# Two column blocks of the third gate among the first projections, and a new place for the modulation's multiply-adds

## The chip, the cores and the metric

One core of a Trainium2 chip runs the whole layer in one launch. The metric is device time in microseconds. TensorE (PE) multiplies and writes to PSUM, VectorE (DVE) and ScalarE (ACT) work elementwise, GpSimd (POOL) does small things, and SyncE (SP) issues nearly all loads.

## The reference

One decoder layer on 256 tokens of width 2048, all in float32. The conditioning vector `c` gives six modulation vectors; the residual stream is normed, scaled and shifted to `h`, and one wide projection of `h` feeds three token mixers and three gates:

```python
mod = (jax.nn.silu(c) @ w_ada[l] + b_ada[l]).reshape(B, N_MOD, 1, D)
sh1, sc1, gt1, sh2, sc2, gt2 = (mod[:, j] for j in range(N_MOD))
h = rmsnorm(x, g_mix[l]) * (1.0 + sc1) + sh1
z = h @ w_in[l]
(mq, mk, mv, mo, mi, mf, dq, dk, dv, sq, sk, sv, gm, gd, gs) = split_cols(z, IN_SIZES)
...
merged = (jax.nn.sigmoid(gm) * (out_m @ w_branch[l, 0])
          + jax.nn.sigmoid(gd) * (out_d @ w_branch[l, 1])
          + jax.nn.sigmoid(gs) * (out_s @ w_branch[l, 2]))
x = x + gt1 * (merged @ w_out[l])
...
x = x + gt2 * ((jax.nn.silu(gate) * hid[..., D_FF:]) @ w_down[l])
```

`gs`, 2048 columns wide, is the third gate: it weighs the stick-breaking branch. `h` needs the first two modulation vectors, `sh1` and `sc1`, and so 2048 x 4096 numbers of `w_ada` (33.6 MB) ahead of the first whole projection.

## The kernel before

**Exact products.** A float32 factor is split into a high part (a cast on ACT) and a low part (a subtraction on DVE); each product is three matmuls, high x high, high x low and low x high. `weights` (L338) loads a raw chunk of up to four k tiles (128 rows each) by 512 columns, 1 MB, casts `hi` (L349) and subtracts `lo` (L351), two k tiles at a time. `gemm` (L357) runs over chunks and calls `tick` (L209) between them. Raw chunks come from a pool of three buffers, with a fourth added while `state["spare"]` is set (`raw_tile`, L217); the modulation's raw tiles come from the same pool.

**The modulation as partial sums.** Because `h` for a k tile needs only its own rows of `sh1` and `sc1`, the vectors are made in portions: two k tiles, two more (`ada_first`, L259), then three quads of four (`ada_quad`, L280). In a portion DVE multiplies rows of `w_ada` by the conditioning value and adds them up (`ada_mac`, L225: L230 starts a sum, L232 adds), PE sums over partitions (L248), and `make_h` (L465) scales the normed `x` to `h` on ACT and splits it. These steps are generators in the queue `ada`: each `next` is one step, and in a quad one step is one multiply-add of 128 x 1024.

**The first projections.** Thirteen column blocks (`first`, L515) are worked on with whatever k tiles of `h` exist: `visit(cis, kt1, rate)` (L568) brings each block in `cis` up to k tile `kt1` by `partial` (L528). A block begun before is copied back from SBUF into PSUM ("put", L545) or its new sum is added by DVE (L558); a piece not finished is copied out (L556). Blocks 0 and 1 stay in PSUM (`kept`). `rates["ada"]` and `rates["side"]` say how many steps of each queue a tick runs; `partial` also runs steps until the `h` that it needs has been made. After the visits come the last k tiles of each block (L901), with stick-breaking in the queue `side` after block 5; then the third gate's four column blocks by `gates` (L857), two before and two after the drain of that queue.

**What sets the order.** Loads go out on SP in the order of the program. On PE, DVE and ACT the framework places instructions by a simulated timeline, with program order as priority; `tc.issue_after(ins)` puts the block's instructions behind `ins` on its engine. `state["split"]` is the latest low-part subtraction in program order, `state["load"]` the latest weight load. `ada_late` (L294) already puts its multiply-adds behind `state["split"]`.

Of the kernel before, what the change touches and what calls it, by code (L numbers as in the profile page):

```python
# [10 lines left out]
F32 = mybir.dt.float32  # L11
F32R = mybir.dt.float32r
AF = mybir.ActivationFunctionType
# [4 lines left out]
P = 128  # L18
S = 256
# [16 lines left out]
C_GM, C_GD, C_GS = 10248, 12296, 14344  # L36
# [3 lines left out]
def kernel(  # L40
# [14 lines left out]
    adap = ctx.enter_context(tc.tile_pool(name="adap", bufs=3))  # L55
# [7 lines left out]
    def slot(i, name):  # L63
        n = NT * MH * (MDH + 1) + 8 if i == 2 else 2048
        return slots.tile([P, n], F32, tag=f"s{i}", name=name)
# [4 lines left out]
    def wide(name):  # L70
        return tmp.tile([P, 512], F32, tag="wide", name=name, bufs=3)

    def sidewide(name):
        return tmp.tile([P, 512], F32, tag="sidewide", name=name, bufs=4)

    def small(name):
        return tmp.tile([P, 256], F32, tag="small", name=name, bufs=3)

    V, A, T = nc.vector, nc.scalar, nc.tensor
# [111 lines left out]
    side = deque()  # L191
    ada = deque()
    state = {"ada": 0.0, "side": 0.0, "split": None, "load": None, "hold": None, "h": 0, "spare": None}
# [13 lines left out]
    rates = {"ada": 0.0, "side": 1.0}  # L207

    def tick():  # L209
        for key, queue in (("ada", ada), ("side", side)):  # L210
            state[key] += rates[key]
            n = int(state[key])
            state[key] -= n
            pump(queue, n)
# [10 lines left out]
    def ada_mac(accs, raw, kt0, nk):  # L225
        for k in range(nk):
            kt = kt0 + k
            acc = accs[kt % len(accs)]
            if kt < len(accs):
                V.tensor_scalar(acc, raw[:, k, :], ccol[:, kt:kt + 1], None, ALU.mult)  # L230
            else:
                state["mac"] = V.scalar_tensor_tensor(acc, raw[:, k, :], ccol[:, kt:kt + 1], acc, ALU.mult, ALU.add)  # L232
# [47 lines left out]
    def ada_quad(k0, acc):  # L280

        for q in range(8):
            raw = raw_tile(2, 1024, "raw4")
            for i in range(2):
                r0, c0 = q * 256, i * D + k0 * P
                with tc.issue_after(state["load"].ins):
                    nc.sync.dma_start(raw[:, :, i * 512:(i + 1) * 512],
                                      w_ada[r0:r0 + 256, c0:c0 + 512].rearrange("(k p) f -> p k f", p=P))
            for k in range(2):
                ada_mac([acc], raw[:, k:k + 1, :], 2 * q + k, 1)  # L290
                yield
        ada_sums([acc], k0, 4)

# [38 lines left out]
    a1 = const.tile([P, KD], F32, name="a1")  # L332
    b1 = const.tile([P, KD], F32, name="b1")
# [89 lines left out]
    def split(hi, lo, src):  # L423

        A.copy(hi, src)  # L425
        return V.tensor_tensor(lo, src, hi.bitcast(F32), ALU.subtract)


    h1 = [slots.tile([P, KD // 2, 2 * S], F32R, tag=t, name="h1") for t in ("hh", "hl")]
# [3 lines left out]
    xnT_k = lambda kt: xnT[kt // 8][:, (kt % 8) * S:(kt % 8 + 1) * S]  # L433
# [29 lines left out]
            A.copy(xnT[k2 // 4][:, (k2 % 4) * 512:(k2 % 4 + 1) * 512], pb)  # L463

    def make_h(kt0, kt1):  # L465
        ts = []
        for kt in range(kt0, kt1):
            t = small("ht")
            ts.append(t)
            hi, lo = hact[0](kt), hact[1](kt)  # L470
            if kt0 == 0:
                A.activation(hi, xnT_k(kt), AF.Identity, scale=a1[:, kt:kt + 1], bias=b1[:, kt:kt + 1])
                V.tensor_scalar(t, xnT_k(kt), a1[:, kt:kt + 1], b1[:, kt:kt + 1], ALU.mult, ALU.add)
                state["split"] = V.tensor_tensor(lo, t, hi.bitcast(F32), ALU.subtract)
            else:
                A.activation(t, xnT_k(kt), AF.Identity, scale=a1[:, kt:kt + 1], bias=b1[:, kt:kt + 1])
                state["split"] = split(hi, lo, t)
        if kt0 == 0:
            state["first"] = state["split"]
        state["h"] = kt1  # L480
# [19 lines left out]
    def dest_D(i):  # L500
        def f(b):
            pieces = []
            for lo_, hi_, t in ((0, 8, None), (8, 1032, dq), (1032, 2056, dk), (2056, 3080, dv)):
                s_, e_ = max(lo_, i * 440), min(hi_, (i + 1) * 440)
                if s_ >= e_:
                    continue
                if t is None:
                    d = zif[:, b, s_:e_]
                else:
                    d = t[:, b * MW + s_ - lo_:b * MW + e_ - lo_]  # L510
                pieces.append((slice(s_ - i * 440, e_ - i * 440), d))
            return pieces
        return f

    first = []  # L515
# [5 lines left out]
        first.append(("T", C_SV + ch * 512, 512, dest_T(sv, ch), 1.0))  # L521
    for i in range(7):
        first.append(("T", C_IF + 440 * i, 440, dest_D(i), 1.0))

    def shaped(src, dst):
        return src.rearrange("p (a b) -> p a b", a=dst.shape[1]) if len(dst.shape) == 3 else src

    def partial(ci, kt0, kt1):  # L528
        orient, col0, n, dest, scale = first[ci]
        while state["h"] < kt1:  # L530
            pump(ada, 1)
        if kt0 == 0 and ci == 0:
            state["first"], done = state["mac0"], state["first"]
        pin = kt0 == 0 and ci < 2
        if kt0 == 0 and ci < 2:
            kept[ci] = [bank("kept"), bank("kept")]
        acc = kept.get(ci)


        put = acc is None and 0 < kt0 and kt1 < KD and not (kt1 == 4 and ci in (6, 8))  # L540
        if put:
            acc = [gp.tile([P, 512], F32, tag="gp", name="gp") for _ in range(2)]
            for b in range(2):
                for cs, d in dest(b):
                    A.copy(shaped(acc[b][:, cs], d), d)  # L545
        acc = gemm(orient, hact, w_in, 0, col0, n, kt0, kt1, hold=state["first"] if pin else None, hold_all=pin,
                   acc=acc)
        if kt0 == 0 and ci == 0:
            state["first"] = done
        for b in range(2):  # L550
            for cs, d in dest(b):
                if ci in kept:
                    if kt1 == KD:
                        A.activation(d, shaped(acc[b][:, cs], d), AF.Copy, scale=scale)
                elif put or kt0 == 0:
                    A.copy(d, shaped(acc[b][:, cs], d))  # L556
                else:
                    V.scalar_tensor_tensor(d, shaped(acc[b][:, cs], d), scale, d, ALU.mult, ALU.add)  # L558
        tick()

    kept = {}
# [1 line left out]
    quads = slot(4, "quads")  # L563
    ada.append(ada_first(2))
    ada.extend(ada_quad(k0, quads[:, (i % 2) * 1024:(i % 2 + 1) * 1024]) for i, k0 in enumerate((4, 8, 12)))
    done = [0] * 13

    def visit(cis, kt1, rate):  # L568
        rates["ada"] = rate
        for ci in cis:  # L570
            partial(ci, done[ci], kt1)
            done[ci] = kt1

    visit(range(0, 9), 2, 0.62)
    visit(range(9, 13), 4, 1.9)
    visit(range(0, 9), 4, 1.0)
    side.append(late_vectors())
    rates["side"] = 0.4
    visit(range(0, 10), 8, 1.72)
    visit(range(10, 13), 12, 1.36)  # L580
    visit(range(0, 7), 12, 1.36)
    drain(ada)
    drain(side)
    state["spare"] = None
# [270 lines left out]
    mg = []  # L855

    def gates(col_g, ch, dst):  # L857
        acc = gemm("T", hact, w_in, 0, col_g + ch * 512, 512, 0, KD)
        for tt in range(NT):
            A.activation(dst[tt], acc[tt], AF.Sigmoid)  # L860
        tick()

    def mg_of(ch):
        o = (ch % 2) * 512
        return [mg[ch // 2][:, tt * 1024 + o:tt * 1024 + o + 512] for tt in range(NT)]
# [31 lines left out]
        yield from ada_columns(4, bsc2_c, a2, gffn_c)  # L897

    ada.append(ada_rest())
    rates["side"] = 2.4  # L900
    for ci in range(13):  # L901
        partial(ci, done[ci], 16)
        if ci == 5:
            side.append(stick())


    rates["side"] = 2.0
    rates["ada"] = 0.9
    mg.append(slot(8, "mg0"))
    for ch in range(2):  # L910
        gates(C_GS, ch, mg_of(ch))
    drain(side)
    mg.append(slot(9, "mg1"))
    side.append(diff())
# [8 lines left out]
    for ch in range(2):  # L923
        acc = gemm("T", hact, w_in, 0, C_MO + ch * 512, 512, 0, KD)
# [6 lines left out]
    for ch in range(2):  # L931
        acc = gemm("T", hact, w_in, 0, C_MV + ch * 512, 512, 0, KD)
# [5 lines left out]
    for t, col0, f0 in ((mqT, C_MQ, 0), (mkT, C_MK, 8)):  # L938
        for ch in range(2):
            acc = gemm("H", h1act, w_in, 0, col0 + ch * 512, 512, 0, KD)  # L940
# [44 lines left out]
    for ch in range(4):  # L985
        acc = gemm("T", mact, w_out, 0, ch * 512, 512, 0, KD)
        cs = slice(ch * 512, (ch + 1) * 512)
        for tt in range(NT):
            t = wide("t512")
# [15 lines left out]
        for tt in range(NT):  # L1005
# [5 lines left out]
            with tc.issue_after(m.ins) if last else nullcontext():  # L1011
                for i in range(4):
                    k = 4 * ch + i
                    m = T.transpose(pbs[i // 2][:, (i % 2) * S + tt * P:(i % 2) * S + (tt + 1) * P],
                                    x2[tt][:, k * P:(k + 1) * P], ident)
        for i in range(4):
            k = 4 * ch + i
# [13 lines left out]
    k = 0  # L1031
    while k < KD:
# [4 lines left out]
        for j in range(m):  # L1037
            b = b2[:, k + j:k + j + 1]
            hi, lo = h2act(k + j)[:, 0:S], h2act(k + j)[:, S:2 * S]
# [9 lines left out]
    for half, (c0, c1) in enumerate(((0, 6), (6, NCH))):  # L1049
# [37 lines left out]
        for n in range(4):  # L1087
            acc = gemm("T", act, w_down, c0 * 512, n * 512, 512, 0, 4 * (c1 - c0))
# [37 lines left out]
```

## Time and profile before

| | |
|---|---|
| median of 3 runs | 1785.43 us (1785.31 to 1785.56) |
| profiled execution | 1786.68 us |
| its span | 1785.0 us |
| PE busy | 1762.3 us (99%) |
| DVE busy | 1302.2 us (73%) |
| ACT busy | 954.2 us (53%) |
| HBM read | 419.68 MB, 236 GB/s over the span |

The span runs from the first to the last instruction of the profiled execution. Busy time of PE is a union of matmuls with modelled ends. DVE and ACT are no bound by their totals; what they hold up is read where PE waits.

### The profile page before, as it was taken

The numbers are of one execution on the slowest core, as the hardware profiler recorded it, in microseconds if no ns is written. First come the engines' busy times: TensorE is split into PE (matmuls) and PEld (weight loads), VectorE is DVE, ScalarE is ACT, GpSimd is POOL, SyncE is SP. The second block draws the span as 40 slices with busy tenths as digits, with TensorE's granted clock in tenths as the row PEclk, the third lists the DMA queues.
The fourth block names the chain that finished last, engine by engine and source line by source line (L and its number), as shares of the span: only waits on it lengthen the run. The fifth ranks groups of instructions, "written<-read, shape, count | busy, mean of one in ns | idle before, by whom it ended". The sixth has DMA issues, their size and how long they took to land.

```text
span 1785.0 us, 23783 instructions
## 1 busy us (share of the span) xinstructions
PE 1762.3 (99%) x9168; PEld 1514.4 (85%) x9168; DVE 1302.2 (73%) x1734; ACT 954.2 (53%) x1338; POOL 16.7 (1%) x44
## 2 busy tenths in 40 slices
PE   7989999999999999999999999999999999999998
PEld 6889999888778888888888888888888888888887
DVE  6878656888878688777986577888875556666654
ACT  6667555676566566544444555555553345555432
POOL 2000000000000000000000000000000000000000
PEclk9999999999999999999999999999999999999999
DMA  9989755867767667688996557777765555555563
GB/s 330 361 315 336 281 175 166 281 223 250 252 232 260 212 219 252 230 281 285 323 307 212 185 165 247 258 258 268 267 202 201 191 189 189 189 189 189 189 214 116
DMA packets 219730, 423.33 MB, mean 237 GB/s; under 512 B 9026, under 2 KB 31674, under 8 KB 219104
## 3 DMA queue, kind: packets, MB, share of 16 engines
q1 hardware_dynamic: 217328, 417.44, 68.6%
q0 software_dynamic: 1008, 2.23, 0.4%
q10 hardware_dynamic: 1280, 2.14, 0.3%
q8 instruction: 72, 1.18, 0.3%
q14 instruction: 42, 0.34, 0.1%
HBM read 419.68 MB, written 2.10 MB: 236 GB/s over the span
## 4 chain that ended last, share of the span: by engine, by line
PE 96%; DMA 2%; DVE 1%; ACT 0%; issue 0%; SPq 0%; DVEq 0%
PE gp L398 55%; PE acch L384 32%; PE gp L403 2%; PE kept L403 2%; DMA raw<-in_w_ada_dram 1%; PE psc L688 1%; DMA raw<-in_w_in_dram 0%; PE pm L248 0%; DVE quads L232 0%; SPq L271 0%; PE pr L329 0%; DVE lo L351 0%; PE pa L713 0%; PE pm L238 0%; PE pmg L886 0%
## 5 line engine op out<-in xcount | busy, mean ns | idle before, releaser
L351 DVE TENSOR_TENSOR lo<-raw,hi 128x1024 fp32r<-128x1024 f32 (+1 forms) x608 | 724.8, 1208 | 363.0 <-ACT hi L349 325.9
L349 ACT CAST hi<-raw 128x1024 fp32r<-128x1024 f32 (+1 forms) x608 | 619.2, 1039 | 551.0 <-PE gp L398 348.7
L398 PE MATMUL gp<-hi,h 128*128 128x512 f32 (+1 forms) x1600 | 412.5, 386 | 2.1 <-ACT hi L349 1.0
L384 PE MATMUL acch<-h,hi 128*128 128x512 f32 x1664 | 403.6, 391 | 0.2 <-DVE h L1041 0.2
L384 PEld LDWEIGHTS acch<-h,hi 128*128 128x128 f32 x1664 | 303.4, 188 | 58.3 <-DVE h L1041 1.1
L398 PEld LDWEIGHTS gp<-hi,h 128*128 128x128 f32 x1600 | 295.8, 188 | 54.9 <-ACT hi L349 2.8
L398 PE MATMUL gp<-lo,h 128*128 128x512 f32 (+1 forms) x800 | 228.3, 383 | 0.0
L384 PEld LDWEIGHTS acch<-h,lo 128*128 128x128 f32 x1664 | 217.3, 191 | 10.8
L384 PE MATMUL acch<-h,lo 128*128 128x256 f32 x1664 | 220.8, 282 | 0.0
L232 DVE SCALAR_TENSOR_TENSOR acc<-araw,ccol,acc 128x512 f32<-128x512 f32 x240 | 179.0, 746 | 2.8 <-DMA araw<-in_w_ada_dram 1.1
L398 PEld LDWEIGHTS gp<-lo,h 128*128 128x128 f32 x800 | 149.7, 188 | 25.3 <-issue 0.3
L398 PE MATMUL gp<-hi,atl 128*128 128x512 f32 x352 | 137.0, 389 | 0.0
L398 PE MATMUL gp<-hi,ath 128*128 128x512 f32 x352 | 136.9, 389 | 0.0
L398 PE MATMUL gp<-lo,ath 128*128 128x512 f32 x352 | 105.8, 389 | 0.0
L398 PEld LDWEIGHTS gp<-lo,ath 128*128 128x128 f32 x352 | 66.1, 188 | 13.8
L398 PEld LDWEIGHTS gp<-hi,ath 128*128 128x128 f32 x352 | 66.1, 188 | 13.8
L398 PEld LDWEIGHTS gp<-hi,atl 128*128 128x128 f32 x352 | 66.0, 188 | 13.7
L232 DVE SCALAR_TENSOR_TENSOR quads<-raw,ccol,quads 128x1024 f32<-128x1024 f32 x45 | 57.7, 1281 | 11.1 <-DMA raw<-in_w_ada_dram 10.6
L398 PE MATMUL gp<-hi,mgl 128*128 128x512 f32 x128 | 50.3, 393 | 0.0
L398 PE MATMUL gp<-hi,mgh 128*128 128x512 f32 x128 | 50.0, 392 | 0.0
L1066 DVE SCALAR_TENSOR_TENSOR y<-gsum,cols,y 128x255 f32<-128x255 f32 (+1 forms) x88 | 41.4, 478 | 3.3 <-ACT y L1064 2.9
L403 PE MATMUL kept<-h,hi 128*128 128x256 f32 x256 | 39.1, 290 | 2.9 <-ACT h L425 1.1
(365 smaller groups left out, 1605.3 us busy)
## 6 DMA issues: line engine op xcount, KB each, us to landing
raw<-in_w_in_dram SPq DMA_DIRECT2D x98, 1024.0 KB, 5.1
raw<-in_w_up_dram SPq DMA_DIRECT2D x88, 1024.0 KB, 5.1
araw<-in_w_ada_dram SPq DMA_DIRECT2D x128, 512.0 KB, 5.9
raw<-in_w_down_dram SPq DMA_DIRECT2D x44, 1024.0 KB, 5.1
raw<-in_w_ada_dram SPq DMA_DIRECT2D x62, 512.0 KB, 7.4
raw<-in_w_branch_dram SPq DMA_DIRECT2D x24, 1024.0 KB, 6.3
raw<-in_w_in_dram SPq DMA_DIRECT2D x25, 880.0 KB, 5.6
raw<-in_w_out_dram SPq DMA_DIRECT2D x16, 1024.0 KB, 5.0
```

Of the source, the lines that this page charges most:

```text
L232: state["mac"] = V.scalar_tensor_tensor(acc, raw[:, k, :], ccol[:, kt:kt + 1], acc, ALU.mult, ALU.add)
L349: A.copy(hi[:, :, :n], raw[:, k0:k0 + 2, :n])
L351: state["split"] = V.tensor_tensor(lo[:, :, :n], raw[:, k0:k0 + 2, :n], hi[:, :, :n].bitcast(F32), ALU.subtract)
L384: T.matmul(acc[t][:, 0:m], lhsT=w[k // 2][:, k % 2, sl], rhs=ah(s0 + k)[:, 0:m], start=start, stop=s0 + k == kt1 - 1 and w is (wh if flip ...
L398: T.matmul(o, lhsT=a(s0 + k)[:, sl], rhs=wk[:, :n], **kw)
L403: T.matmul(o, lhsT=wk[:, sl], rhs=a(s0 + k), **kw)
L688: T.matmul(pcs[cc][:, o], lhsT=qT[cp, qs], rhs=kT[cp, ks], start=True, stop=True)
L1066: V.scalar_tensor_tensor(yf[:, sft:S], src[:, 0:S - sft], wc(2 - sft), yf[:, sft:S], ALU.mult, ALU.add)
```

## The change

**Multiply-adds.** Those of a quad are put behind the latest split. **make_h.** From the second portion on it works on pairs of k tiles: two scalings on ACT into one tile of the pool "sidewide" (four places of 512 columns, in place of "small", three of 256), then one cast and one subtraction for both. **Third gate.** Its first two column blocks become blocks 13 and 14 of `first`; their sums between visits lie in one tile of the pool "acc" and three of "wide", and after the last k tile DVE adds and ACT writes the sigmoid to `mg`. **Visits and rates.** The lists of visits and the rates of the queue `ada` are new, blocks 10 to 12 stop at k tile 8 where they went to 12, and block 6 too. The last k tiles of block 13 stand between blocks 5 and 6, those of block 14 at the end, and the queue `ada` runs from block 5 on at rate 0.5.

```diff
--- before.py
+++ after.py
@@ -287,7 +287,8 @@
                     nc.sync.dma_start(raw[:, :, i * 512:(i + 1) * 512],
                                       w_ada[r0:r0 + 256, c0:c0 + 512].rearrange("(k p) f -> p k f", p=P))
             for k in range(2):
-                ada_mac([acc], raw[:, k:k + 1, :], 2 * q + k, 1)
+                with tc.issue_after(state["split"].ins):
+                    ada_mac([acc], raw[:, k:k + 1, :], 2 * q + k, 1)
                 yield
         ada_sums([acc], k0, 4)
 
@@ -463,18 +464,20 @@
             A.copy(xnT[k2 // 4][:, (k2 % 4) * 512:(k2 % 4 + 1) * 512], pb)
 
     def make_h(kt0, kt1):
-        ts = []
-        for kt in range(kt0, kt1):
-            t = small("ht")
-            ts.append(t)
+        for kt in range(kt0, kt1, 1 if kt0 == 0 else 2):
             hi, lo = hact[0](kt), hact[1](kt)
             if kt0 == 0:
+                t = small("ht")
                 A.activation(hi, xnT_k(kt), AF.Identity, scale=a1[:, kt:kt + 1], bias=b1[:, kt:kt + 1])
                 V.tensor_scalar(t, xnT_k(kt), a1[:, kt:kt + 1], b1[:, kt:kt + 1], ALU.mult, ALU.add)
                 state["split"] = V.tensor_tensor(lo, t, hi.bitcast(F32), ALU.subtract)
             else:
-                A.activation(t, xnT_k(kt), AF.Identity, scale=a1[:, kt:kt + 1], bias=b1[:, kt:kt + 1])
-                state["split"] = split(hi, lo, t)
+                t = sidewide("ht")
+                for j in range(2):
+                    A.activation(t[:, j * S:(j + 1) * S], xnT_k(kt + j), AF.Identity, scale=a1[:, kt + j:kt + j + 1],
+                                 bias=b1[:, kt + j:kt + j + 1])
+                both = h1[kt // 8][:, kt % 8:kt % 8 + 2, :]
+                state["split"] = split(both[:, :, 0:S], both[:, :, S:2 * S], t.rearrange("p (k s) -> p k s", k=2))
         if kt0 == 0:
             state["first"] = state["split"]
         state["h"] = kt1
@@ -521,6 +524,9 @@
         first.append(("T", C_SV + ch * 512, 512, dest_T(sv, ch), 1.0))
     for i in range(7):
         first.append(("T", C_IF + 440 * i, 440, dest_D(i), 1.0))
+    gsp = []
+    for ch in range(2):
+        first.append(("T", C_GS + ch * 512, 512, lambda b, ch=ch: [(slice(0, 512), gsp[ch][b])], 1.0))
 
     def shaped(src, dst):
         return src.rearrange("p (a b) -> p a b", a=dst.shape[1]) if len(dst.shape) == 3 else src
@@ -556,6 +562,8 @@
                     A.copy(d, shaped(acc[b][:, cs], d))
                 else:
                     V.scalar_tensor_tensor(d, shaped(acc[b][:, cs], d), scale, d, ALU.mult, ALU.add)
+                    if ci > 12:
+                        A.activation(mg_of(ci - 13)[b], d, AF.Sigmoid)
         tick()
 
     kept = {}
@@ -563,7 +571,7 @@
     quads = slot(4, "quads")
     ada.append(ada_first(2))
     ada.extend(ada_quad(k0, quads[:, (i % 2) * 1024:(i % 2 + 1) * 1024]) for i, k0 in enumerate((4, 8, 12)))
-    done = [0] * 13
+    done = [0] * 15
 
     def visit(cis, kt1, rate):
         rates["ada"] = rate
@@ -572,13 +580,14 @@
             done[ci] = kt1
 
     visit(range(0, 9), 2, 0.62)
-    visit(range(9, 13), 4, 1.9)
-    visit(range(0, 9), 4, 1.0)
+    gsp.extend([[adap.tile([P, 512], F32, tag="acc", name="gsp", bufs=2), wide("gsp")], [wide("gsp"), wide("gsp")]])
+    visit(range(9, 15), 4, 1.4)
+    visit(range(0, 9), 4, 1.15)
     side.append(late_vectors())
     rates["side"] = 0.4
-    visit(range(0, 10), 8, 1.72)
-    visit(range(10, 13), 12, 1.36)
-    visit(range(0, 7), 12, 1.36)
+    visit([13, 14, *range(0, 10)], 8, 1.55)
+    visit([*range(10, 13)], 8, 1.55)
+    visit([13, 14, *range(0, 6)], 12, 1.55)
     drain(ada)
     drain(side)
     state["spare"] = None
@@ -897,18 +906,16 @@
         yield from ada_columns(4, bsc2_c, a2, gffn_c)
 
     ada.append(ada_rest())
-    rates["side"] = 2.4
-    for ci in range(13):
+    mg.append(slot(8, "mg0"))
+    for ci in (*range(6), 13, *range(6, 13)):
         partial(ci, done[ci], 16)
         if ci == 5:
             side.append(stick())
-
-
-    rates["side"] = 2.0
-    rates["ada"] = 0.9
-    mg.append(slot(8, "mg0"))
-    for ch in range(2):
-        gates(C_GS, ch, mg_of(ch))
+            rates["ada"], rates["side"] = 0.5, 2.6
+
+
+    rates["ada"], rates["side"] = 0.9, 2.0
+    partial(14, done[14], 16)
     drain(side)
     mg.append(slot(9, "mg1"))
     side.append(diff())
```

## Rows read from the trace of the kernel before

**Rows 1.** by stretches: busy us (count) per engine, granted clock, DMA share, GB/s

```profile
25.00:125.00 100.00, 92.74 (x585) 85.16 (x585) 83.04 (x105) 61.73 (x101) 0.00 (x0) 0.98 0.96 337
50.00:75.00 25.00, 23.96 (x126) 21.68 (x125) 21.25 (x25) 16.02 (x30) 0.00 (x0) 1.00 1.03 370
125.00:200.00 75.00, 75.00 (x424) 69.89 (x423) 59.80 (x60) 52.40 (x92) 0.00 (x0) 1.00 0.95 340
200.00:235.00 35.00, 35.00 (x244) 32.91 (x243) 18.08 (x21) 23.84 (x39) 0.00 (x0) 1.00 0.61 208
235.00:325.00 90.00, 90.00 (x523) 84.30 (x522) 60.96 (x86) 47.31 (x56) 0.00 (x0) 1.00 0.57 189
```

**Rows 2.** timeline of PE: start, us, instruction, count [idle before <-releaser]

```profile
49.13 0.47 PE L398 MATMUL gp<-hi,h 128*128 128x440 f32 x1 [0.19 <-ACT hi L349]
...
55.71 0.47 PE L398 MATMUL gp<-hi,h 128*128 128x440 f32 x1 [0.18 <-ACT hi L349]
...
58.30 0.67 PE L398 MATMUL gp<-hi,h 128*128 128x440 f32 x2 [0.49 <-ACT h L425]
59.34 1.26 PE L398 MATMUL gp<-hi,h 128*128 128x440 f32 x5 [0.36 <-DVE h L426]
...
89.58 2.11 PE L398 MATMUL gp<-hi,h 128*128 128x512 f32 x8 [0.67 <-ACT hi L349]
...
102.09 0.44 PE L398 MATMUL gp<-hi,h 128*128 128x440 f32 x1 [0.21 <-DVE dq L558]
...
108.63 0.50 PE L403 MATMUL kept<-h,hi 128*128 128x256 f32 x2 [1.08 <-ACT h L425]
110.10 2.05 PE L403 MATMUL kept<-h,hi 128*128 128x256 f32 x15 [0.97 <-ACT hi L349]
...
120.03 1.24 PE L403 MATMUL gp<-h,hi 128*128 128x256 f32 x9
123.56 0.50 PE L403 MATMUL gp<-h,lo 128*128 128x256 f32 x2 [2.29 <-DVE lo L351]
123.90 1.00 PE L403 MATMUL gp<-h,hi 128*128 128x256 f32 x7
```

**Rows 3.** chain that ended last, in order: start, us, work, count

```profile
195.46 11.51 PE kept L403 x96
...
1319.44 128.75 PE gp L398 x568
```

**Rows 4.** timeline of DVE, two stretches

```profile
57.66 1.28 DVE L232 SCALAR_TENSOR_TENSOR quads<-raw,ccol,quads 128x1024 f32<-128x1024 f32 x1
...
110.75 0.42 DVE L426 TENSOR_TENSOR h<-ht,h 128x256 fp32r<-128x256 f32 x1
...
119.76 2.60 DVE L232 SCALAR_TENSOR_TENSOR quads<-raw,ccol,quads 128x1024 f32<-128x1024 f32 x2 [3.81 <-DMA raw<-in_w_ada_dram]
122.28 3.49 DVE L351 TENSOR_TENSOR lo<-raw,hi 128x1024 fp32r<-128x1024 f32 x3
```

**Rows 5.** timeline of ACT

```profile
100.80 1.59 ACT L476 ACTIVATE ht<-xnT,b,a 128x256 f32<-128x256 f32 x3 [0.62 <-DVE a L256]
...
106.21 0.62 ACT L476 ACTIVATE ht<-xnT,b,a 128x256 f32<-128x256 f32 x1
...
122.49 2.00 ACT L349 CAST hi<-raw 128x1024 fp32r<-128x1024 f32 x2 [5.30 <-DMA raw<-in_w_in_dram]
```

**Rows 6.** timeline of SP, which issues the loads

```profile
100.72 0.88 SPq L287 DMA_DIRECT2D raw<-in_w_ada_dram  x2
109.66 0.37 SPq L344 DMA_DIRECT2D raw<-in_w_in_dram  x1
```

**Rows 7.** by line and shape, 25:235 us, then all: count, busy, mean ns

```profile
L232 DVE SCALAR_TENSOR_TENSOR quads<-raw,ccol,quads 128x1024 f32<-128x1024 f32 x45 | 57.7, 1281 | 11.1 <-DMA raw<-in_w_ada_dram 10.6
L351 DVE TENSOR_TENSOR lo<-raw,hi 128x1024 fp32r<-128x1024 f32 x38 | 45.6, 1221 | 21.1 <-ACT hi L349 16.8 <-PE gp L398 2.5 <-ACT gp L545 1.7
...
L545 ACT COPY gp<-sv 128x512 f32<-128x512 f32 x12 | 7.1, 594 | 0.3
...
L426 DVE TENSOR_TENSOR h<-ht,h 128x256 fp32r<-128x256 f32 x14 | 5.5, 419 | 2.5 <-ACT h L425 2.5
...
L426 DVE TENSOR_TENSOR loA<-spA,hiA 128x512 fp32r<-128x512 f32 x4 | 2.7, 683 | 0.0
```

## The prediction, made before the result was known

> **What bounds the kernel now.** I read the table by stretches first [rows 1]. TensorE (PE) is busy without a break in every stretch from 125 us on, with VectorE (DVE) at 52 to 80%; only 25 to 125 us, with DVE at 83%, has PE idle, 100 - 92.74 = 7.26 us. The granted clock there is 0.98 and 1.00 in the stretches after it, so the clock is not what is lost. The kernel is bound by PE's own instructions, which the change leaves as they are in number and shape: the two column blocks need 2 x 16 x 6 matmuls of 512 columns whether they run alone at the end or in pieces. At the steady pitch [rows 3] of 128.75 / 568 = 0.227 us a visit of four k tiles (24 matmuls) is 5.44 us, one of two is 2.72 us; with 256 columns the pitch is 11.51 / 96 = 0.120 us.
>
> So all that can be won is PE's waiting between its first projection and 125 us. I read that in the timeline of PE, as idle time in brackets [rows 2]: 0.19 + 0.18 + 0.49 + 0.36 + 0.67 + 0.21 + 1.08 + 0.97 + 2.29 = 6.44 us in nine waits. The brackets are short, because ends of matmuls are modelled and overlap the next start: the piece at 120.03 has nine matmuls, 9 x 0.12 us, so the next was due at 121.11 and came at 123.56, a loss of 2.45 for a bracket of 2.29; and the two after it take 0.34 us to the next row where 0.24 was due. So each wait costs about 0.16 + 0.10 us more than its bracket: 6.44 + 9 x 0.26 = 8.8 us, 0.5% of the time. That is the ceiling of the gain.
>
> **What the waits are.** The timelines of DVE, ACT and SP at these places tell three causes.
> (a) Order on DVE. At 119.76 two multiply-adds of the modulation stand at DVE's head, idle 3.81 us for their own transfer, and three splits (low parts of weights, L351) start only after them at 122.28 [rows 4]; PE waits for such a low part until 123.56. At 57.66 a multiply-add runs ahead of the low parts of h for k tiles 2 and 3, and PE waits at 58.30 and 59.34 for just these.
> (b) The making of h for k tiles 4 to 7. Three of the four scaled tiles are written by 102.4, the fourth only at 106.21 [rows 5], because the buffer "small" has three places and a low part had to be finished first; the last low part of h ends at 110.75 + 0.42 [rows 4]. PE wants it at 107.4 (108.63 - 1.08 - 0.16): the wait at 108.63 is for the fourth cast of h, the one at 110.10 for a cast of weights which, I read, ACT ran behind these.
> (c) Buffers of raw weights. SP issues nothing from about 101.6 to 109.66 [rows 6], as the next buffer is held by a split that has not run; ACT then waits 5.30 us for that transfer at 122.49 [rows 5], which is the other half of the wait at 123.56.
>
> **The change part by part.**
> 1. Multiply-adds behind the latest split (L291). Nothing is added; DVE's order becomes that of the loads: split, multiply-add, split. It covers the 45 multiply-adds of 1.28 us [rows 7] and the three that start a sum. At 57.66 one of 1.28 us leaves the way of h, which is worth most of 0.49 + 0.36 + 2 x 0.26 = 1.37; I take 1.0. At 123.56 the low part whose high part was ready before 119.76 no longer stands behind the multiply-adds; PE then runs its low-part matmuls from 121.1 and waits next for the high parts cast from 122.49, due about 0.6 us after it runs dry. Of 2.29 + 0.26 I take 1.9. The price: a multiply-add may now stand behind a split that waits for its cast, so its buffer is given back later. Bounds: from 0 to the rival below.
> 2. Pairs in make_h. Per pair of k tiles the two casts and two low parts of 256 columns (low part 0.419 us) become one of 512 (0.683) [rows 7]: on DVE 2 x 0.419 - 0.683 = 0.16 us less per pair, seven pairs, 1.1 us in all, and off PE's way. The two scalings stay as they are. What counts is the buffer: four places of twice the width, so no scaling waits for a low part. In (b) that is up to 106.21 - 102.4 = 3.8 us earlier, against a lateness of 1.08 + 0.97 + 2 x 0.26 = 2.57.
> 3. Two blocks more in the first visits, and lower rates. One step of the modulation's queue is one multiply-add; each quad needs 16, and h for k tiles 4 to 7 is made at step 21 (4 + 16, and one to close). Before, the visits give 9 x 0.62 + 4 x 1.9 + 9 x 1.0 = 22.2 steps, and step 21 falls on the eighth of the last nine visits, one visit (2.7 us) ahead of the need. Afterwards it is 9 x 0.62 + 6 x 1.4 + 9 x 1.15 = 24.3; step 21 falls on the seventh, 5.4 us ahead. With part 2 the lateness has two covers, each as long as itself, so I take all 2.57. For k tiles 8 to 11 step 37 falls on the ninth of fifteen visits, and six visits, some 30 us, are left; before it was the ninth of ten (22.2 + 9 x 1.72 = 37.7), one left.
> DVE's load per visit, at 512 columns throughout, with splits at 1.22 and multiply-adds at 1.28 us: in the long visits to k tile 4, 2 x 1.22 + 1.9 x 1.28 = 4.87 of 5.44 us before, 4.23 after; in the short ones 1.22 + 1.28 = 2.50 of 2.72 before, 1.22 + 1.15 x 1.28 = 2.69 after, which is full; in the visits to k tile 8, 4.64 before, 4.42 after. So of the smaller waits (0.19, 0.18, 0.67, 0.21, with 4 x 0.26 a sum of 2.29) I take 0.6 back, no more: the short visits get no easier.
> 4. Upkeep of the two blocks: per block two evacuations after the first visit and two copies into PSUM with two out of it for each of two more, 10 x 0.59 us on ACT [rows 7], and two DVE adds of about 0.69 at the end (the row of 512 columns, 0.683). For both, 12 us on ACT and 3 on DVE. ACT is idle for 30% or more of these stretches [rows 1], and DVE's 3 us fall where it is at 68%. Sigmoids only move. PE sees nothing: I take 0. If the cover fails, the cost is one copy ahead of a visit, 4 visits x 0.59 = 2.4 us; below nothing it cannot be.
> 5. Later: the modulation's rest starts one projection earlier, at rate 0.5, in 15 visits beside stick-breaking. Some 8 steps of two multiply-adds, under 1.5 us each, 12 us on DVE in about 90: from 68% to 81%, about the 80% at which PE lost nothing from 125 to 200 us [rows 1]. Stick-breaking has 28 steps; 15 ticks x 2.6 = 39 hold them, so the drain after block 14 is empty. I take 0; bounds 0 and about 2 us (one wait like that at 123.56). SP's queue gets no new DMA, only the two blocks' weights earlier, and the gp tile with three PSUM banks turns over as in the other blocks.
>
> Sum: 1.0 + 1.9 + 2.57 + 0.6 = 6.1 us won, nothing paid. The profiled execution took 1786.68 us (span 1785.00 and 1.68 around it), 1.25 above the median of 1785.43; what I subtract lies inside the span, so it holds for the median: 1785.43 - 6.1 = 1779.3. With all of 8.8 it is 1776.6; the forecast's own range is 1776.0 to 1781.8.
>
> **The rivals.**
> Transfers set the pace. For it: the DMA share is 0.96 from 25 to 125 us, and the two blocks bring 2 x 1.05 MB of weights ahead of the second h; short visits ask (0.52 + 1.15 x 0.52) MB / 2.72 us = 415 GB/s. Against: the long visits before them drop from 376 to 328 (1.05 MB and 1.4 steps of 0.52 MB in 5.44 us), the best stretch moved 370 at share 1.03 [rows 1], and the stop at 101.6 to 109.66 was a buffer, not the DMA engines. Then only the lateness of h goes and the rest of the waits is found again elsewhere: 1785.43 - 2.57 = 1782.9, between 1781.9 and 1785. Beside it stands a rule of the Trainium skill, HBM Reference, Specifications (TRN2): about 358 GB/s per core as its share, some 425 for a core streaming alone. By 358 the sum would be this rival's 2.57 us, by 425 the forecast's; the 370 of the stretch from 50 to 75 us [rows 1] contradicts 358 as a limit here, and no row shows 425.
>
> Slower: multiply-adds pinned behind splits hold the raw buffers. Weights and modulation share four buffers in the order of the loads. A pinned multiply-add waits for a split, which waits for a cast on ACT (mean idle before a split of 1024 columns 21.1 / 38 = 0.6 us [rows 7]), which can stand behind a PSUM copy; if each of the 24 raw tiles of the quads keeps its buffer 0.6 us longer, that is 14 us, and with DVE full in the short visits nothing catches up. Less a gain of 6 to 9 us this is 5 to 8 us slower: about 1792. It decides from a mean delay of 8.8 / 24 = 0.37 us. Against it: PE lost nothing from 125 to 200 us with DVE at 80%, and the load of the long visits falls.
>
> No effect: the waits are set by ACT's order (a cast behind an evacuation that waits for PE), they move but stay: 1785.4, within 2 us.
>
> **How the numbers follow.** Forecast 0.57, transfers 0.22, no effect 0.08, slower 0.13. A difference of 0.2% (3.6 us) is about what a measurement can tell here. Faster by more: 0.57; within: 0.22 + 0.08 + 0.02 of the slow rival = 0.32; slower by more: 0.11. The range for 8 in 10 goes from 1776.0 (all waits gone) to 1785.7 (transfers and half of no effect); out are most of the slow rival and the other half.
>
> **What would show it.** Right: in the stretch 25 to 135 us PE's idle falls from about 7 to under 3 us; no wait for h of k tiles 4 to 7; no multiply-add of the quads idle on its transfer with a ready split behind it; PE at 100% from 135 us on as before. Part 2: four scalings in a row on ACT. Transfers: ACT's casts wait longer for raw weights, with share near 1. Slow rival: new waits of PE for low parts between 60 and 200 us, and SP waiting for DVE's multiply-adds. Wrong altogether: PE idle after 135 us, or another number of matmuls.

## The result, and the profile after

The changed kernel takes 1794.13 us (median of 6 runs, 1793.17 to 1795.23) against 1785.37 us: ratio 1.0048, 95% interval 1.0037 to 1.0059. It is slower by 8.8 us where 6.1 us less were forecast. The profiled execution after took 1793.17 us with a span of 1791.5, the fastest of its six, and that of before was 1.3 us above its median; so the two traces differ by 6.5 us of span, and what follows accounts for these 6.5.

The table by stretches, after (columns as in [rows 1]):

```profile
25.00:125.00 100.00, 96.03 (x549) 85.46 (x549) 82.61 (x102) 65.81 (x107) 6.64 (x13) 1.00 0.97 335
125.00:200.00 75.00, 73.33 (x438) 66.98 (x436) 54.33 (x53) 51.01 (x91) 0.00 (x0) 1.00 0.90 317
200.00:235.00 35.00, 34.71 (x247) 32.71 (x248) 24.29 (x24) 24.45 (x36) 0.00 (x0) 1.00 0.82 299
325.00:425.00 100.00, 96.07 (x457) 83.47 (x456) 83.20 (x114) 63.82 (x71) 0.00 (x0) 0.98 0.64 223
```

Where PE lost time before, it loses less: idle from 25 to 125 us falls from 7.26 to 3.97 us. But 1.67 us of idle are new between 125 and 200 us, and 3.93 us between 325 and 425 us, a stretch that had none. DVE's share is nearly what it was.

The timeline of PE, after: the start of the first projection, then the waits (columns as in [rows 2]), with the first output matmul of stick-breaking (`po`) and the transposes (`ptf`) of the differential attention's result, which follow the drain ahead of the mLSTM values:

```profile
26.85 0.73 PE L404 MATMUL kept<-h,hi 128*128 128x256 f32 x4 [0.42 <-ACT h L471]
...
54.06 0.47 PE L399 MATMUL gp<-hi,h 128*128 128x440 f32 x1 [1.14 <-ACT hi L350]
...
56.70 0.47 PE L399 MATMUL gp<-hi,h 128*128 128x440 f32 x1 [0.57 <-ACT hi L350]
...
58.05 0.87 PE L399 MATMUL gp<-hi,h 128*128 128x440 f32 x3 [0.17 <-ACT h L426]
59.40 0.87 PE L399 MATMUL gp<-hi,h 128*128 128x440 f32 x3 [0.48 <-DVE h L427]
...
109.36 1.07 PE L399 MATMUL gp<-hi,h 128*128 128x440 f32 x4 [0.42 <-ACT gp L551]
...
119.06 2.14 PE L399 MATMUL gp<-hi,h 128*128 128x512 f32 x8 [0.77 <-ACT gp L551]
...
188.52 1.90 PE L399 MATMUL gp<-hi,h 128*128 128x440 f32 x8 [0.27 <-ACT hi L350]
...
200.29 2.13 PE L399 MATMUL gp<-hi,h 128*128 128x512 f32 x8 [1.58 <-ACT hi L350]
...
315.74 0.59 PE L650 MATMUL po<-ez,sv 128*128 128x256 f32 x2
...
400.68 0.71 PE L399 MATMUL gp<-lo,h 128*128 128x512 f32 x2
405.32 2.07 PE L399 MATMUL gp<-hi,h 128*128 128x512 f32 x4 [3.93 <-ACT mg L869]
407.19 1.05 PE L399 MATMUL gp<-lo,h 128*128 128x512 f32 x2
...
564.91 1.91 PE L757 MATMUL ptf<-ident,od 128*128 128x128 f32 x16
567.98 1.20 PE L399 MATMUL gp<-hi,h 128*128 128x512 f32 x4 [1.16 <-ACT mv L941]
```

The early waits from 54.06 on answer to [rows 2]: eight, 5.40 us in brackets, by the same reckoning 5.40 + 8 x 0.26 = 7.5 us against 8.8. The waits for h at 108.63 and 110.10 and for the low part at 123.56 are gone, but 188.52 and 200.29 are new. The big one is at 405.32: PE wants a PSUM bank which ACT has not emptied. ACT's timeline, after, tells why; its first row answers to [rows 5]:

```profile
103.94 2.08 ACT L477 ACTIVATE ht<-xnT,b,a 128x256 f32<-128x256 f32 x4 [0.29 <-DVE a L256]
...
400.96 0.59 ACT L426 CAST osh<-po 128x512 fp32r<-128x512 f32 x1 [3.92 <-PE po L652]
401.45 1.91 ACT L663 ACTIVATE dsq<-dq 128x2048 f32<-128x2048 f32 x1
403.38 1.28 ACT L869 ACT_TABLE_LOAD   x1
404.67 1.09 ACT L869 ACTIVATE mg<-gp 128x512 f32<-128x512 f32 x2
```

The four scalings of h for k tiles 4 to 7 now run in a row. At 400.96 ACT casts the last output of stick-breaking, for which it idled 3.92 us, then runs the first Square of the differential attention, loads a table, and only then takes the third gate's sigmoids that empty PE's banks. And the rows of before to set beside the first projection, `po` and `ptf` above:

```profile
27.83 1.22 PE L403 MATMUL kept<-h,hi 128*128 128x256 f32 x4 [0.82 <-ACT h L472]
...
301.87 0.59 PE L641 MATMUL po<-ez,sv 128*128 128x256 f32 x2
...
556.95 0.60 PE L748 MATMUL ptf<-ident,od 128*128 128x128 f32 x4
```

Stick-breaking's first output comes 13.87 us later, `ptf` 7.96 us later. Between the first projection and `ptf` lies the place where the time went; the experiments were needed to see whether the wait on ACT or the late chain is the cause.

The first row of each kernel tells something else. In the changed kernel the first projection starts 0.98 us earlier, and its first 18 matmuls take 2.24 us (26.85 to 29.09) where they took 3.51 us before (27.83 to 31.34). In the trace of before the granted clock was 0.57 from 27 to 31 us; in the trace after it was 1.00.

### The profile page after: what moved, and what is told of

It is laid out like the page before. It is cut to its first block, busy times and chain, and to the rows that moved or that the text cites. A ratio compares the mean times of both kernels' runs of the same rounds, so it can differ in the third digit from the quotient of the medians.

```text
span 1791.5 us, 23764 instructions
## 1 busy us (share of the span) xinstructions
PE 1765.0 (99%) x9168; PEld 1514.2 (85%) x9168; DVE 1303.5 (73%) x1731; ACT 961.4 (54%) x1344; POOL 16.4 (1%) x44
## 4 chain that ended last, share of the span: by engine, by line
PE 92%; DMA 4%; ACT 2%; DVE 1%; issue 1%; SPq 0%; ACTq 0%; DVEq 0%
PE gp L399 52%; PE acch L385 32%; DMA raw<-in_w_in_dram 3%; PE kept L404 2%; PE gp L404 2%; ACT hi L350 1%; PE psc L697 1%; DMA raw<-in_w_ada_dram 0%; DMA x<-in_x_dram 0%; DVE lo L352 0%; PE pm L248 0%; PE spin L186 0%; DVE quads L232 0%; ACT x L452 0%; PE pr L330 0%
## 5 line engine op out<-in xcount | busy, mean ns | idle before, releaser
L1086 ACT COPY usum<-acch 128x256 f32<-128x256 f32 x44 | 16.3, 372 | 41.2 <-PE acch L385 41.2
```

The source lines that it names most:

```text
L1086: A.copy(uf, accu[2 * b + f][:, S:2 * S])
```

## The experiments

Medians of 4 to 11 runs, each beside runs of the kernel before on the same chip; "ratio" is to those. The theories are named in the expectations as they came up: A, the gate's sigmoid behind the Square on ACT; B, the pinned multiply-adds; C, the chain of the two attentions, formed after A fell.

| run | median us | before, us | ratio (95%) |
|---|---|---|---|
| pin alone | 1792.80 | 1785.61 | 1.0038 (1.0026 to 1.0051) |
| pairs alone | 1784.18 | 1785.61 | 0.9990 (0.9981 to 0.9999) |
| blocks alone | 1794.42 | 1785.61 | 1.0041 (1.0029 to 1.0054) |
| changed, DVE empties the gate | 1794.40 | 1785.61 | 1.0051 (1.0038 to 1.0063) |
| changed, cover given back | 1786.65 | 1786.21 | 1.0002 (0.9993 to 1.0011) |
| that without pin | 1783.92 | 1786.21 | 0.9990 (0.9981 to 0.9998) |
| before, stick-breaking after block 7 | 1793.18 | 1786.21 | 1.0040 (1.0025 to 1.0055) |
| pin to weight splits | 1787.55 | 1786.21 | 1.0004 (0.9995 to 1.0013) |
| before, stick-breaking after block 6 | 1786.32 | 1786.81 | 0.9997 (0.9988 to 1.0006) |
| still more cover, no pin | 1786.64 | 1786.81 | 0.9998 (0.9989 to 1.0007) |
| changed, one head left out | 1788.52 | 1786.81 | 1.0009 (1.0000 to 1.0018) |
| blocks alone, cover given back | 1783.32 | 1786.61 | 0.9983 (0.9974 to 0.9992) |

**Pin alone.** Added to the kernel before:

```diff
-                ada_mac([acc], raw[:, k:k + 1, :], 2 * q + k, 1)
+                with tc.issue_after(state["split"].ins):
+                    ada_mac([acc], raw[:, k:k + 1, :], 2 * q + k, 1)
```

> The kernel before with one edit of the change: the quads' multiply-adds stand behind the latest split. Theory A (the loss is the third gate's sigmoid, which the two moved blocks put behind the differential attention's first Square on ACT: PE waits 3.9 us for a PSUM bank at 401 us and runs at half clock for some 3 us after it): no such wait here; the early waits shrink by some 2 us, so 1783 to 1785.5 us. Theory B (pinned multiply-adds hold the raw buffers): 3 us or more slower, 1788 to 1793, with new waits of PE between 100 and 205 us.

The time is theory B's, 7 us slower by itself; there is no wait at 401 us, as theory A said, but its 1783 to 1785.5 us are missed. The timelines of PE, DVE and SP in this run show how:

```profile
171.26 1.76 PE L399 MATMUL gp<-hi,h 128*128 128x440 f32 x8
172.85 0.96 PE L399 MATMUL gp<-lo,h 128*128 128x440 f32 x4
...
173.86 0.96 PE L399 MATMUL gp<-lo,h 128*128 128x440 f32 x4
179.88 3.14 PE L399 MATMUL gp<-hi,h 128*128 128x440 f32 x8 [5.06 <-ACT hi L350]
```

```profile
169.12 0.42 DVE L427 TENSOR_TENSOR h<-ht,h 128x256 fp32r<-128x256 f32 x1
169.45 0.75 DVE L230 TENSOR_SCALAR quads<-raw,ccol 128x1024 f32<-128x1024 f32 x1
170.24 6.57 DVE L232 SCALAR_TENSOR_TENSOR quads<-raw,ccol,quads 128x1024 f32<-128x1024 f32 x5
```

```profile
163.07 0.88 SPq L287 DMA_DIRECT2D raw<-in_w_ada_dram  x2
174.19 0.37 SPq L345 DMA_DIRECT2D raw<-in_w_in_dram  x1
```

`make_h` sets `state["split"]` too, so the next quad's multiply-adds stand behind the last low part of h, which ends at 169.12 + 0.42. Six of them then run without a pause. Until the first are done their raw buffers are not free, SP issues nothing from 163.95 to 174.19, and PE runs dry at 174.8 and waits 5.06 us for weights.

**Pairs alone.** `make_h` of the change in the kernel before.

> The kernel before with make_h in pairs alone. Theories A and B agree: the scalings of k tiles 4 to 7 run in a row, the wait of 2.6 us for h at 107 to 110 us goes or shrinks, 1782.5 to 1785 us. If pairs alone bring the wait at 401 us, theory A is wrong about which edit causes it.

1.4 us faster, at the low end of what was expected, but not by the way expected. PE's timeline here:

```profile
108.92 0.62 PE L403 MATMUL kept<-h,hi 128*128 128x256 f32 x3 [2.46 <-DVE h L426]
```

The scalings ran in a row, yet PE waited 2.46 us for h at the same place. The low parts of k tiles 6 and 7 now come as one, and on DVE they stand behind a multiply-add (from 105.85) and a split of weights (from 107.04):

```profile
108.18 0.68 DVE L426 TENSOR_TENSOR h<-ht,h 128x512 fp32r<-128x512 f32 x1
```

The wait at 123.56 [rows 2] is gone, but others grew: from 45 to 125 us PE's brackets add up to 6.59 us, against 6.44 before. What is won is ahead of them. The first projection starts at 26.67 in place of 27.83, and so it does, between 26.5 and 26.9, in every kernel here that has the pairs, while those without start at 27.7 to 28.0. In the rows thirteen small loads by POOL, whose tiles lie in "sidewide" too, are issued from 25.55 us on, in place of 3.76 to 11.94 us, and DVE gets its second tile of `w_ada` at 15.09 in place of 16.43; that the one is the reason for the other was not tested.

**Blocks alone.** The change without pin and pairs.

> The two column blocks, the visits and rates alone, without the pinned multiply-adds and without pairs. Theory A: the wait at about 400 us with the half clock behind it is here (5 to 6 us lost), the early stretch gains 2 to 5 us: 1786 to 1790 us, slower than before. Theory B: no pinned multiply-adds, so no loss; faster than before, 1778 to 1782 us.

About as slow as the whole change. Early it had only four waits (0.19, 0.19, 0.52 and 1.42 us, or 3.4 us by the reckoning above): 5.4 us won, nearly the forecast. All of it and more was lost later (7 us more by the ratio, 5.0 by the spans of the two traces), most of it at the same wait on ACT (3.93 us, at 401.8 us) and at the drain, where four waits add up to 2.47 us.

**The sigmoid's bank emptied by DVE.** In `gates`, for the third gate:

```diff
+            if col_g == C_GS:
+                V.tensor_copy(dst[tt], acc[tt])
-            A.activation(dst[tt], acc[tt], AF.Sigmoid)
+            A.activation(dst[tt], dst[tt] if col_g == C_GS else acc[tt], AF.Sigmoid)
```

> The changed kernel with one thing different: in gates of the third gate DVE copies the sum out of PSUM and ACT takes the sigmoid of the copy in place, so that PE's bank no longer waits for ACT. Theory A: no wait at 401 us and no half clock after it, 5 to 6 us less than the changed kernel: about 1788.3 us. Theory B, or a loss spread over the new visits: 1794 us as before this edit, within 1.

This felled theory A. The wait at 401 us shrank to 0.32 us, and the time did not change, because PE then waited elsewhere. PE's and DVE's timelines of this run:

```profile
555.72 0.60 PE L238 MATMUL pm<-ident,acc 128*128 128x128 f32 x4
562.58 3.87 PE L757 MATMUL ptf<-ident,od 128*128 128x128 f32 x16 [6.26 <-DVE od L745]
```

```profile
561.21 2.36 DVE L745 TENSOR_TENSOR od<-od,ro 128x1024 f32<-128x1024 f32 x2
```

PE came to `ptf` 6.26 us before the normalised result. In the changed kernel the wait on ACT had hidden this: there the same DVE instructions end at 562.56 + 2.35 = 564.91, the moment at which `ptf` starts. Its DVE timeline:

```profile
562.56 2.35 DVE L745 TENSOR_TENSOR od<-od,ro 128x1024 f32<-128x1024 f32 x2
```

So taking the wait at 401 us away gives nothing. Stick-breaking and differential attention are one long chain of small steps, released by block 5 and due at the drain ahead of the mLSTM values. The visits of the change put 24 k-tile pieces of 512 columns (1.36 us each) ahead of its start in place of 16 of 440 (six matmuls at 0.2 us, from the rows at 171.26 and 172.85 above: 1.2 us): 32.6 - 19.2 = 13.4 us of PE's work that no longer covers the chain. Its first output came 13.87 us later. This is theory C.

**Cover given back.** In the changed kernel blocks 13 and 14 stop at k tile 8, so eight of these pieces come behind the chain's start:

```diff
-    visit([13, 14, *range(0, 6)], 12, 1.55)
+    visit(range(0, 6), 12, 1.55)
```

> The changed kernel, but blocks 13 and 14 stop at k tile 8 in the visits, so that 8 k-tile pieces (10.9 us of PE) come after stick-breaking has begun and not before. Theory C (stick-breaking and differential attention are one chain of about 283 us, released by block 5 and due at the drain ahead of the mLSTM values; the change took 10.9 us of PE's work from between them): stick-breaking starts near 270 us, the wait at the drain (1.2 us and more) goes, 1783 to 1787 us against 1794. Theory A alone (the sigmoid behind the Square): unchanged if the two still meet on ACT, 1792 to 1794.

8 us less than the changed kernel, by the ratios 1.0002 against 1.0048, and the meeting on ACT at 401 us is gone as well. The wait at the drain was to go too, but 1.15 us of it stay behind `ptf`. PE's timeline:

```profile
302.97 0.59 PE L650 MATMUL po<-ez,sv 128*128 128x256 f32 x2
...
558.05 1.91 PE L757 MATMUL ptf<-ident,od 128*128 128x128 f32 x16
561.11 1.19 PE L399 MATMUL gp<-hi,h 128*128 128x512 f32 x4 [1.15 <-ACT mv L941]
```

**The same without the pin.**

> As the run with the cover given back, but the quads' multiply-adds are not pinned (blocks and pairs stay). Theories B and C together: the early stretch loses 5 to 6.5 us instead of 11.9, no wait at the drain: 1779 to 1782 us, faster than before. If the pin does no harm beside the new rates, as the run with the cover given back, within 1 us.

The pin's diff is undone on top of the last one. Faster than before, by 2.3 us where 4 to 7 were expected: between 125 and 200 us PE is idle for 0.91 us in place of 1.67, and from 25 to 125 us hardly less than in the changed kernel (3.65). The waits near 119 and 200 us are not there without the pin; one of 0.91 us at 176.15 is new.

**The kernel before with stick-breaking late.** Nothing of the change, only:

```diff
-        if ci == 5:
+        if ci == 7:
             side.append(stick())
```

> The kernel before, with stick-breaking let into its queue after block 7 in place of block 5: 12 k-tile pieces (4 + 8 of 440 columns, 14.5 us of PE) less between its start and the drain, and nothing else of the change. Theory C: PE waits there for what the cover lacks, 14.5 less some 3 us of slack: 8 to 13 us slower, 1794 to 1798 us. If the loss belongs to the new blocks and visits: 1785.5 us, within 1.5.

7 us slower, just under the expected range. PE's timeline:

```profile
315.49 0.59 PE L641 MATMUL po<-ez,sv 128*128 128x256 f32 x2
...
407.46 2.08 PE L398 MATMUL gp<-hi,h 128*128 128x512 f32 x4 [4.39 <-ACT mg L860]
...
564.78 1.91 PE L748 MATMUL ptf<-ident,od 128*128 128x128 f32 x16
```

`po` and `ptf` stand within 0.3 us of where the changed kernel has them, and the same wait on ACT for the third gate's sigmoid appears, with none of the new visits. That is most of the change's loss (7.0 of 8.8 us) made in the kernel before, by delay alone.

**Pinned to weight splits.** As the pin alone, with a second name set only in `weights`:

```diff
+                state["wsplit"] = state["split"]
...
+                with tc.issue_after(state["wsplit"].ins):
```

> The kernel before with the quads' multiply-adds pinned behind the latest split of a weight chunk only, not behind the last low part of h. Theory B in its narrower form (the pin costs because make_h sets the latest split too, and the next quad's multiply-adds then wait for h): no wait of 5 us near 175 us, 1783 to 1786.5 us against 1792.8 with the full pin. If pinning to any split costs: 1789 us or more.

The loss of the pin is gone (1.0004 against 1.0038), so it was the low part of h. But nothing is won either: the interval holds no change, and the median is 1 us above the expected range.

**Stick-breaking after block 6.**

> The kernel before with stick-breaking let in after block 6 in place of block 5: 4 k-tile pieces of 440 columns (4.8 us) less between its start and the drain. From the first output matmul of stick-breaking to the transposes behind the drain the chain takes 247.9 to 250.6 us in the four runs where PE waits for it and 255 where it does not: some 5 to 6 us of slack in the kernel before. Theory C: within the slack, no loss: 1785 to 1787.5 us, against 7 us lost for 14.5 us of delay. If the loss is simply in proportion to the delay: 2.3 us slower, about 1788.5.

No loss: the chain has slack before it costs. The test is weaker than planned, since `po` came 2.6 us later, not 4.8: in proportion to the run with block 7 (7.0 us for a `po` 13.62 us later) that would be 1.3 us or 1.0007, just outside the interval. That `ptf` starts at 556.95, as in the kernel before, speaks for the slack.

**Still more cover.** Blocks 13 and 14 are left out of the visits to k tile 8 as well.

> The faster variant (blocks and pairs, no pin, cover given back) with still more cover: blocks 13 and 14 stop at k tile 4 in the visits, so another 8 k-tile pieces (10.9 us) move behind the start of stick-breaking. Theory C: past the chain's length more cover buys nothing but the 1.2 us wait for the mLSTM values at the drain; the early visits have less to do beside the loads of the modulation and may lose 1 to 3 us again: 1782.5 to 1786 us. If cover were worth its time in proportion: 1777 or less.

No gain, and 0.6 us above the expected range. `ptf` came at 541.50 without a wait at the drain, but PE waited early instead, for h of the last k tiles:

```profile
225.39 4.85 PE L403 MATMUL kept<-h,hi 128*128 128x256 f32 x23 [4.44 <-ACT h L425]
```

**One head left out.** In `diff` head 7 is skipped and its values copied through.

> The changed kernel with head 7 of the differential attention left out (its values are copied through instead), 1.5 us or so of PE's work. Theory C: the chain is shorter by one head, 12 to 14 us, so the wait at the drain goes: 6 to 9 us less than the changed kernel, 1785 to 1788 us. If the loss lies in the new visits and evacuations, only the left-out work goes: 1791.5 to 1793 us.

Between the two expectations, just above C's range. The drain's wait went, but the wait on ACT stayed; stick-breaking's first output, at 314.82, had hardly moved against the changed kernel:

```profile
404.40 2.08 PE L399 MATMUL gp<-hi,h 128*128 128x512 f32 x4 [3.93 <-ACT mg L870]
```

So a shorter chain takes away the wait at the drain and leaves the one on ACT; giving the cover back takes away the one on ACT and leaves 1.15 us at the drain.

**Blocks alone, cover given back.**

> The blocks, visits and rates alone (no pin, no pairs), with the cover given back as in the faster variant. With the blocks alone PE waits four times between 45 and 235 us (0.19, 0.19, 0.52 and 1.42 us), some 5 us less in all than in the kernel before, but the chain behind the stick-breaking took it back. Theory C: with the chain covered this gain is left, 1780 to 1783 us. If the early gain is lost elsewhere, as the 1.2 us at the drain and new early waits: 1783 to 1786 us.

3.3 us faster than before, just inside the second range, and the lowest median of all, 0.6 us under the run without the pin. The executions of both kernels that had the same mean granted clock differ by 2.0 us or more too (at 1.000: 1782.0 against 1784.5 us). The 1.2 us at the drain are there (557.17). PE's waits between 45 and 235 us, from its timeline:

```profile
47.80 0.47 PE L398 MATMUL gp<-hi,h 128*128 128x440 f32 x1 [0.20 <-ACT hi L349]
...
54.37 0.46 PE L398 MATMUL gp<-hi,h 128*128 128x440 f32 x1 [0.19 <-ACT hi L349]
...
56.96 1.34 PE L398 MATMUL gp<-hi,h 128*128 128x440 f32 x5 [0.52 <-ACT h L425]
...
61.42 0.47 PE L398 MATMUL gp<-hi,h 128*128 128x440 f32 x1 [1.41 <-DVE h L426]
```

## Why the prediction was wrong

The step that failed is part 5, and what it should have set against part 3. "Stick-breaking has 28 steps; 15 ticks x 2.6 = 39 hold them, so the drain after block 14 is empty. I take 0; bounds 0 and about 2 us." That counts steps in the order of the program. The chain is bound by its own waits: from `po` to `ptf` it took 247.9 us in the run where PE waited longest for it, and 255.1 in the kernel before. It had some 7 us to spare and lost 13.87 us of cover, so `ptf` had to come later by about 7; it came 7.96 later. The rates behind block 5 were not varied by themselves, but the run with the cover given back has them too and loses nothing. I took no row of that chain into the argument, only the busy shares of the engines beside it.

Point by point:

- Ceiling and place of the early gain: right in sum. With the blocks alone PE lost 3.4 us instead of 8.8, nearly the 6.1 us that were forecast, and with the cover given back 3.3 us of this reach the median. (The spans of the two traces differ by 4.7, but 1.3 of them are the slow start of the first projection in the trace of before.) That the sum fits is luck: the pin, which was to bring 2.9 of it, and the pairs, which were to share in 2.57, are not in these runs. New visits and rates alone took away every wait from 89.58 on.
- "So the clock is not what is lost": wrong for this trace. The 0.98 from 25 to 125 us is the 0.57 from 27 to 31 us, and it cost 1.3 us that are no part of the 8.8.
- Part 1, taken as 2.9 us won: wrong in sign, 7 us lost by the pin alone, and 2.7 with the cover given back (1786.65 against 1783.92). The slow rival had the mechanism (raw buffers held) and a chance of 0.13, but not the reason, that the latest split may be h's. In the whole change the pin cannot have been the main cause: the blocks alone are about as slow.
- Part 2: the four scalings run in a row as said, which alone did not end PE's wait for h. The pairs won 1.4 us by another way, as far as their trace shows: a start 1.16 us earlier, which the prediction did not have; that the time fell into the range expected for them was luck.
- Part 3: h for k tiles 4 to 7 comes in time, as said. In the whole change the early waits still fell only from 8.8 to 7.5 us, since pin and pairs brought others than they took. Those at 119.06 and 200.29 came with the pin, as the run without it does not have them.
- Part 4: at nothing, and nothing was seen against it except the 0.42 and 0.77 us that PE waited for copies into PSUM (109.36 and 119.06), and 1.20 and 0.91 us in the run without the pin.
- Transfers as the limit: no. The early gain of the blocks alone came with a DMA share of 0.98 from 25 to 125 us, against 0.96 before.

Of the 6.5 us of span, 2.2 us are won up to the last matmul of block 3, which comes 11.2 us later with 13.4 us of work put ahead of it. All of that is the first projection, which starts 0.98 us earlier and runs at the full clock (1.27); of the early waits nothing reaches this point, though by the reckoning 1.3 us should. The wait on ACT with its slow matmuls takes about 5.5, the wait behind `ptf` 1.4; some 2 us are in pieces that I did not follow. That profile and median differ by 2 us is the spread of single executions, of which the last section shows a part.

## What to carry to other kernels

When work is moved ahead of the point that releases a long chain of small steps, it no longer covers that chain: measure the chain from its release to its deadline, set it against the busy engine's work between the two points, and count the move against the difference. Busy shares do not show this, since an engine can be at 100% up to the deadline with little to spare. A wait that is taken away within such a stretch gives nothing if the chain is due just behind it.

And an order tied to "the latest" of something should name which: here one name served weights and activations, and the pin to the wrong one cost 7 us. Before a difference of 1 or 2 us between two traces is given a cause, read the granted clock of the same stretch in both.

## What the runs showed of the hardware

The granted clock fell to 0.50, the lower of its two levels (1.2 GHz), when PE took up work after its idle time of 3.93 us, and came back within 4 us. Stretches of the changed kernel, columns as in [rows 1]:

```profile
405.30:407.30 2.00, 1.98 (x5) 1.60 (x6) 0.38 (x1) 0.46 (x1) 0.00 (x0) 0.50 0.00 0
407.30:409.30 2.00, 2.00 (x8) 1.62 (x7) 0.79 (x1) 1.87 (x2) 0.00 (x0) 0.73 0.00 0
409.30:420.00 10.70, 10.70 (x48) 8.84 (x48) 10.10 (x11) 8.85 (x9) 0.00 (x0) 1.00 0.45 156
```

The four matmuls from 405.32 took 1.87 us to the next row where 0.91 was due, and the twelve up to 409.59 took 4.27 us where twelve alike took 2.72 from 395.83 on. So this wait cost some 1.5 us more than its length. The eight matmuls of 512 columns from 200.29, behind a wait of 1.58 us, ran 2.13 us, as [rows 2] has it for eight at 89.58 (2.11).

Short waits are no safe sign of the full clock, though, and the same waits in the same code did not always end the same way. In the trace of before the first projection, behind 0.82 us of idle time, got 0.57 from 27 to 31 us (four matmuls in 1.22 us, shown above); in the run with the blocks alone and the cover given back it got 1.00 behind 0.84 us, and in the run with the blocks alone, the same kernel up to there, 0.69. The row at 1.00:

```profile
27.75 0.74 PE L403 MATMUL kept<-h,hi 128*128 128x256 f32 x4 [0.84 <-ACT h L472]
```

And where the kernel before has fifteen matmuls in 2.05 us at 110.10 [rows 2], the run with stick-breaking after block 6, which is the same kernel up to there, has

```profile
110.55 3.44 PE L403 MATMUL kept<-h,hi 128*128 128x256 f32 x15 [0.96 <-ACT hi L349]
```

with a granted clock of 0.50 from 111 to 113 us. The next row stands at 113.82, so this cost 3.27 - 15 x 0.12 = 1.5 us. So two traces can differ by one such loss or two with no difference in the program. The times of single executions go the same way: of the 15 runs of the kernel before beside the last experiment, the two with a mean clock of 1.000 took 1784.45 and 1784.58 us, the five with 0.997 took 1787.34 to 1788.47 us.
